# Early feed-forward weights in half-size tiles on the ScalarE queue, five instead of seven expert buffers, early work over all eight expert pairs

## The chip, the cores and the metric

The kernel runs on one core of a Trainium2 chip. The metric is the device time of one execution in microseconds (us). Times of a kernel are the median of several executions; one more execution is profiled, and all rows below come from that one.

## The reference

Two transformer blocks on 256 tokens of 1024 channels, in float32. The part that matters here is a mixture of experts at the end of the first block (16 experts, hidden size 512, two chosen per token) and, at the start of the second block, a feed-forward layer on the 256 context tokens, which do not depend on the first block.

```python
for e in range(N_EXPERTS):
    hidden = jax.nn.silu(xt @ w_exp_gate[e]) * (xt @ w_exp_up[e])
    y = y + combine[:, e:e + 1] * (hidden @ w_exp_down[e])
...
a, b = jnp.split(h @ w_up, 2, axis=-1)
return (jax.nn.silu(a) * b) @ w_down
```

## The kernel before

The stage in question is `moe` (lines 967 to 1031). It takes the tokens of each expert in slots of 64 and works on the experts in eight pairs; pairs are numbered 0 to 7 here. A pair (loop in `experts`, line 1139 on) needs twelve weight chunks of 1 MB: four of the gate, four of the up and four of the down matrices, one of each for expert `a=0` and one for `a=1`. In the profile their tile is `raw`, and their loads stand on the queue of SP (line 214).

For each pair TensorE (PE) runs, in the names of the rows:
- `egu` (line 1152): 32 matmuls, gate and up, in four groups of eight; a group reads two chunks. The matmuls of `a=0` and `a=1` alternate; each uses 64 of the 128 columns of the array, one the lower and one the upper half.
- `es`: ScalarE (ACT) takes the silu (line 1162), VectorE (DVE) the product (line 1163); `ept` (line 1166) transposes it, and DVE copies it to `hT` (line 1169).
- `ey` (line 1178): 16 matmuls, down, in two groups of eight on two chunks each; then ACT and DVE split the result into `y` high and low (lines 232, 233).
- `eo` (lines 1192, 1193): 16 matmuls that scatter `y` back to the tokens.
- in every second pair `gsp` and `gtp` (slot gates), and `xgp` (lines 1108 to 1111), 32 matmuls that gather the next four experts' tokens.

One matmul of `egu` or `ey` in the program is two rows in the profile (512 `egu` rows for 256 matmuls).

Between them stands **early work**: the second part (six of 22 hidden tiles) of the context tokens' feed-forward layer, which is independent of the experts. `early_ffn` (line 1037) is a generator: 24 steps for twelve up tiles (24 matmuls `pab` each) and 8 for the down tiles (18 matmuls `pd` each), 128x256 per matmul. `self.fill(n)` takes n steps. A weight tile is copied to a high part by ACT (line 225) and its rest taken by DVE (line 228) before PE reads it as `w`. Nine steps are taken ahead of pair 0, six in each pair from then on, and what is left in pair 5 (line 1018); after that the early work is done.

After pair 5 comes a loop that is entered only if an expert has more than 64 tokens (`values_load`, line 1022, and the branches after it); with these inputs it is skipped. The chunks of pair 6 that have a buffer are asked for ahead of it.

The order inside each engine is set by a scheduler of the framework, which places the instructions between two branches by its own estimates. A table of what stands where is given below.

Buffers: all weights of the stage share a ring of seven raw buffers of 1 MB (`raw` with 3, `rawm` with 4), experts and early weights alike; two more spare tiles hold chunks of pair 0. A load waits on its queue until the buffer's last reader is done.

Of the kernel before, what the change touches and what calls it, by code (L numbers as in the profile page):

```python
# [8 lines left out]
F32 = mybir.dt.float32  # L9
F32R = mybir.dt.float32r  # L10
I32 = mybir.dt.int32
AF = mybir.ActivationFunctionType
ALU = mybir.AluOpType
# [4 lines left out]
KD = 8  # L18
S = 256
T2 = 512  # L20
EPS = 1e-6
NFF = 22
PARTS = (6, 6, 6, 4)
EARLY = 1
LOOP_AT = 5
AHEAD = 5
FILL = 3
NORM_LAG = ((1, 3, 0, 2), (1, 2, 0, 3))
LATE_LAG = (2, 2)
# [140 lines left out]
class Builder:  # L170
# [796 lines left out]
    def moe(self):  # L967
        nc, I = self.nc, self.I
        V = nc.vector
        self.raw_n, self.raws = 0, 7  # L970
        with self.sub("hn", 1) as Q, self.sub("hide", PARTS[EARLY]) as E, self.sub("moe", 1) as P, \
                self.sub("wspe", 2) as self.wsp, self.sub("moew", 1) as W, self.sub("rawm", 4) as self.raw_more:
            hH = [Q.tile([128, 1024], F32R, name=f"hnH{t}") for t in range(2)]
            hL = [Q.tile([128, 1024], F32R, name=f"hnL{t}") for t in range(2)]
            rs = self.rs
            self.early = self.early_ffn(E)
            self.fill(FILL)
            comb, sel = self.route(self.lg, rs, P)
            self.fill(FILL)
            pp = self.mm("pos")  # L980
            nc.tensor.matmul(pp[:, 0:16], self.before, sel[:, 0, :], start=True, stop=True)
            nc.tensor.matmul(pp[:, 16:32], self.before, sel[:, 1, :], start=True, stop=False)
            nc.tensor.matmul(pp[:, 16:32], self.ones, sel[:, 0, :], start=False, stop=True)
            for t in range(2):
                nc.tensor.matmul(pp[:, 32:48], self.ones, sel[:, t, :], start=(t == 0), stop=(t == 1))
            mc = P.tile([128, 1], F32, name="mc")
            V.tensor_reduce(mc, pp[:, 32:48], AX.X, ALU.max)
            mi = P.tile([128, 1], I32, name="mi")
            V.tensor_scalar(mi, mc, -1.0, None, ALU.add)
            V.tensor_scalar(mi, mi, 6, None, ALU.logical_shift_right)  # L990
            pos = P.tile([128, 2, 16], F32, name="pos")
            V.scalar_tensor_tensor(pos, pp[:, :32].rearrange("p (t e) -> p t e", t=2), 1.0, sel,
                                   ALU.add, ALU.mult)
            V.tensor_scalar(pos, pos, -1.0, None, ALU.add)
            for t in range(2):
                for q in range(2):
                    p = self.a2("hnt")[:, 0, :] if q else self.mm("hnt")
                    for j in range(4):
                        nc.tensor.transpose(p[:, j * 128:(j + 1) * 128],
                                            self.h[:, q * 4 + j, t * 128:(t + 1) * 128], self.ident)  # L1000
                    hi, lo = hH[t][:, q * 512:(q + 1) * 512], hL[t][:, q * 512:(q + 1) * 512]
                    nc.scalar.activation(hi, p, AF.Copy, scale=rs[:, t:t + 1])
                    V.scalar_tensor_tensor(lo, p, rs[:, t:t + 1], hi.bitcast(F32), ALU.mult, ALU.subtract)
            self.fill(FILL)
            self.gates_of_route()
            order = [(p, c) for p in range(8) for c in range(12)]
            ready = {pc: self.expert_chunk(*pc) for pc in order[:AHEAD]}
            self.spare = [P.tile([128, 2048], F32, tag="xg", name="raw", bufs=2),
                          W.tile([128, 2048], F32, tag="y", name="raw")]
            ready.update({pc: self.expert_chunk(*pc) for pc in order[AHEAD:AHEAD + 2]})  # L1010
            self.on_pool = 0
            self.gs = P.tile([128, 8], F32, name="gs")
            pos2 = P.tile([128, 2, 16], F32, name="pos2")
            V.tensor_copy(pos2, pos)
            for p in self.experts(pos, comb, hH, hL, P, W, ready):
                if p != LOOP_AT:
                    continue
                for _ in self.early:
                    pass
                ready.update({(p + 1, c): self.expert_chunk(p + 1, c) for c in range(7)})  # L1020
                with self.tc.issue_after(self.loaded.ins):
                    more = nc.values_load(mi[0:1, 0:1], min_val=0, max_val=3)
                self.raw_loop = self.wsp
                with self.tc.If(more > 0):
                    with self.tc.For_i(0, more, 1):
                        V.tensor_scalar(pos2, pos2, -64.0, None, ALU.add)
                        for _ in self.experts(pos2, comb, hH, hL, P, W, {}):
                            pass
                self.raw_loop = None
            self.raw_more = None  # L1030
        self.pending = self.two_norms(self.sums)

# [1 line left out]
        for _ in range(n):  # L1034
            next(self.early, None)

    def early_ffn(self, E):
        nc, I = self.nc, self.I
        up, dn = I["ffn1_up_2"][0], I["ffn1_down_2"][0]
        f0, nf = sum(PARTS[:EARLY]), PARTS[EARLY]  # L1040
        sl = slice(S, 2 * S)
        hid = []

        def fetch(c):
            c0 = (f0 + 2 * c) * 128
            return [self.rows(up, 0, KD, m + c0, 256) for m in (0, NFF * 128)]

        nxt = fetch(0)
        for c in range(nf // 2):
            cur, nxt = nxt, fetch(c + 1) if 2 * c + 2 < nf else None  # L1050
            for i in range(2):
                p = self.mm("pab")
                for m in range(2):
                    w = self.split_w(cur[m][:, :, i * 128:(i + 1) * 128])
                    for ks in (range(4), range(4, KD)):
                        self.gemm(p[:, m * S:(m + 1) * S], w, self.xact(sl), ks=ks)
                        if m == 0 or ks[0] == 0:
                            yield True
                s, t = self.s512("fs")[:, :S], self.s512("ft")[:, :S]
                nc.scalar.activation(s, p[:, :S], AF.Silu)  # L1060
                nc.vector.tensor_tensor(t, s, p[:, S:], ALU.mult)
                hid.append([E.tile([128, S], F32R, tag=x, name=x) for x in ("eH", "eL")])
                self.split_a(*hid[-1], t)
                yield True
        for dc in range(4):
            v = self.rows(dn, f0 * 128, nf, dc * 256, 256)
            for i in range(2):
                w = self.split_w(v[:, :, i * 128:(i + 1) * 128])
                p = self.mm("pd")[:, :S]
                self.gemm(p, w, lambda f: hid[f])  # L1070
                self.residual(p, 2 * dc + i, 0, 0, 1)
                yield True

    def expert_chunk(self, p, c):
        I = self.I
# [7 lines left out]
    def experts(self, pos, comb, hH, hL, P, W, ready):  # L1083
        nc, I = self.nc, self.I
# [6 lines left out]
        def chunk(p, c):  # L1091
            w = ready.pop((p, c), None)
            return w if w is not None else self.expert_chunk(p, c)
# [47 lines left out]
        for p in range(8):  # L1141
# [4 lines left out]
            for m in range(2):  # L1146
                for kh in range(2):
                    for aa in both:
                        w = {a: chunk(p, m * 4 + kh * 2 + a) for a in aa}
                        for kk in range(4):  # L1150
                            for a in aa:
                                mm(pr[a * 64:a * 64 + 64, m, :],  # L1152
                                   xg[p // 2][:, kh * 4 + kk, es[a] % 4 * 64:es[a] % 4 * 64 + 64], w[a][:, kk, :],
                                   start=(kh == 0 and kk == 0), stop=(kh == 1 and kk == 3))
                    if self.raw_loop is None:
                        self.fill(1)
            if p % 2 == 0:
                slot_gates(p // 2)
# [2 lines left out]
            s = self.s512("es")  # L1161
# [9 lines left out]
            for fh in range(2):  # L1171
                for aa in both:
                    w = {a: chunk(p, 8 + fh * 2 + a) for a in aa}
                    for ff in range(2):
                        f = fh * 2 + ff
                        for n in range(2):
                            for a in aa:
                                mm(y[a * 64:a * 64 + 64, n, :], hT[:, f, a * 64:a * 64 + 64],
                                   w[a][:, ff, n * 512:(n + 1) * 512], start=(f == 0), stop=(f == 3))
                if self.raw_loop is None:  # L1180
                    self.fill(1)
            y2 = W.tile([128, 2, 1024], F32R, tag="y", name="y")
            yH, yL = y2[:, 0, :], y2[:, 1, :]
# [600 lines left out]
```

## Time and profile before

| | us |
|---|---|
| median of 3 runs | 2293.41 (2293.08 to 2294.7) |
| profiled execution | 2290.45 |
| its span, on core 0 | 2288.6 |
| first `egu` of pair 0 | 313.71 |
| last `eo` ahead of the loop | 543.98 |
| first `egu` behind the loop (pair 6) | 558.34 |
| `sums`, behind the last `eo` of pair 7 | 617.86 |

The span is the time between the first and the last instruction on the core. A row of the timeline gives the start, the length, the engine, the line, the operation, what it writes and reads, and how many equal instructions were merged; in brackets stands how long the engine was idle ahead of it and what ended that. Windows give the busy time of each engine in a stretch, the granted TensorE clock as a share of 2.4 GHz, the busy share of the 16 DMA engines and what they moved.

### The profile page before, as it was taken

Reading aid. Unit: us, or ns where it says so; the run is one execution under the profiler, and the core shown is the slowest. Engines: PE = TensorE matmul, PEld = TensorE weight load, DVE = VectorE, ACT = ScalarE, POOL = GpSimd, SP = SyncE. Lnnn points to the kernel's source line nnn. Section 1 sums busy time; section 2 is a strip of 40 time slices with the busy share of each in tenths; the row PEclk is TensorE's granted clock in tenths of the full one; section 3 lists DMA queues with packets and bytes.
Section 4 is the critical chain, followed back from the end, with each engine's and each line's share of the span. In section 5 each row is a group of like instructions: output and inputs, shape, how many; then the busy total and the mean of one; then the engine's idle time right before and its main releaser. Section 6 shows DMA issues by size and latency. Waiting matters only on the chain.

```text
span 2288.6 us, 32426 instructions
## 1 busy us (share of the span) xinstructions
PE 2217.9 (97%) x13295; PEld 1815.5 (79%) x13295; DVE 1439.2 (63%) x2516; ACT 816.5 (36%) x1256; POOL 163.0 (7%) x160
## 2 busy tenths in 40 slices
PE   8999999998899999999999999999999999899998
PEld 8789974643488977877897777789778888879998
DVE  5656842221388778766678777737874335877676
ACT  4554431110132322346642222224222223485443
POOL 0200100000000000330220000001000002312000
PEclk9999999998899999999999999999999999999999
DMA  7673858897946755320135555434653222416551
GB/s 253 214 241 129 275 191 317 320 395 313 367 162 206 230 171 169 93 85 28 56 130 190 192 170 183 139 96 136 194 165 111 87 70 69 113 33 221 185 175 47
DMA packets 273173, 395.91 MB, mean 173 GB/s; under 512 B 18156, under 2 KB 220540, under 8 KB 260604
## 3 DMA queue, kind: packets, MB, share of 16 engines
q1 hardware_dynamic: 272000, 392.33, 50.7%
q8 instruction: 106, 1.74, 0.3%
q0 software_dynamic: 576, 1.18, 0.2%
q14 instruction: 47, 0.39, 0.1%
q10 hardware_dynamic: 444, 0.27, 0.0%
HBM read 392.71 MB, written 1.05 MB: 172 GB/s over the span
## 4 chain that ended last, share of the span: by engine, by line
PE 69%; DVE 5%; ACT 1%; POOL 1%; issue 1%; ACTq 0%; DVEq 0%; POOLq 0%
PE pab L241 12%; PE pab L242 12%; PE pab L243 12%; PE pd L241 6%; PE pd L242 6%; PE pd L243 6%; PE pj L242 1%; PE pj L241 1%; PE pj L243 1%; PE egu L1152 1%; PE aT L1637 1%; PE as L1608 1%; DVE xL L330 1%; PE ao L1654 1%; PE ada_ps L521 1%; PE po L241 1%
## 5 line engine op out<-in xcount | busy, mean ns | idle before, releaser
L225 ACT ACTIVATE w<-raw 128x1024 fp32r<-128x1024 f32 (+2 forms) x432 | 425.7, 990 | 695.2 <-PE pd L243 239.5
L228 DVE TENSOR_TENSOR w<-raw,w 128x1024 fp32r<-128x1024 f32 (+2 forms) x422 | 479.1, 1145 | 184.7 <-ACT w L225 182.8
L242 PE MATMUL pab<-xL,w 128*128 128x512 f32 (+2 forms) x1600 | 552.3, 346 | 2.3 <-DVE xL L330 1.0
L241 PE MATMUL pab<-xH,w 128*128 128x512 f32 (+2 forms) x1600 | 553.2, 346 | 0.2
L243 PE MATMUL pab<-xH,w 128*128 128x512 f32 (+2 forms) x1600 | 552.0, 345 | 1.4 <-POOL w L228 1.4
L241 PEld LDWEIGHTS pab<-xH,w 128*128 128x128 f32 x1600 | 303.3, 190 | 55.4 <-issue 9.9
L243 PEld LDWEIGHTS pab<-xH,w 128*128 128x128 f32 x1600 | 303.2, 190 | 44.4 <-issue 3.2
L242 PEld LDWEIGHTS pab<-xL,w 128*128 128x128 f32 x1600 | 303.2, 190 | 44.1 <-DVE xL L330 2.3
L539 DVE SCALAR_TENSOR_TENSOR acc<-raw,sT,acc 128x512 f32<-128x512 f32 x420 | 284.8, 745 | 0.0
L241 PE MATMUL pd<-hH,w 128*128 128x512 f32 (+1 forms) x800 | 267.8, 337 | 0.1
L242 PE MATMUL pd<-hL,w 128*128 128x512 f32 (+1 forms) x800 | 267.8, 336 | 0.0
L243 PE MATMUL pd<-hH,w 128*128 128x512 f32 (+1 forms) x800 | 267.1, 335 | 0.0
L241 PE MATMUL pj<-xH,w 128*128 128x256 f32 (+1 forms) x816 | 250.7, 309 | 11.1 <-DVE qra L1536 4.7
L242 PE MATMUL pj<-xL,w 128*128 128x256 f32 (+1 forms) x816 | 246.0, 302 | 6.1 <-DVE xL L330 5.3
L243 PE MATMUL pj<-xH,w 128*128 128x256 f32 (+1 forms) x816 | 245.1, 301 | 0.5 <-DVE w L228 0.5
L241 PEld LDWEIGHTS pj<-xH,w 128*128 128x128 f32 x816 | 156.1, 192 | 26.7 <-DVE qra L1536 5.5
L241 PEld LDWEIGHTS pd<-hH,w 128*128 128x128 f32 x800 | 151.8, 191 | 20.1 <-ACT fs L636 3.4
L686 DVE SCALAR_TENSOR_TENSOR h<-pd,gmod,h 128x256 f32<-128x256 f32 x224 | 100.8, 479 | 104.9 <-PE pd L243 104.6
L242 PEld LDWEIGHTS pj<-xL,w 128*128 128x128 f32 x816 | 156.9, 192 | 11.9 <-DVE xL L330 6.6
L243 PEld LDWEIGHTS pd<-hH,w 128*128 128x128 f32 x800 | 152.3, 191 | 16.8 <-issue 1.7
L242 PEld LDWEIGHTS pd<-hL,w 128*128 128x128 f32 x800 | 152.4, 191 | 15.4 <-DVE hL L233 0.2
L243 PEld LDWEIGHTS pj<-xH,w 128*128 128x128 f32 x816 | 156.8, 192 | 5.7 <-DVE w L228 0.8
(388 smaller groups left out, 2490.3 us busy)
## 6 DMA issues: line engine op xcount, KB each, us to landing
raw<-ffn_up SPq DMA_DIRECT2D x94, 1024.0 KB, 5.4
raw<-w_ada SPq DMA_DIRECT2D x72, 1024.0 KB, 5.3
raw<-ffn_down SPq DMA_DIRECT2D x52, 768.0 KB, 4.8
raw<-w_in SPq DMA_DIRECT2D x32, 1024.0 KB, 5.4
raw<-w_exp_gate SPq DMA_DIRECT2D x32, 1024.0 KB, 8.4
raw<-w_exp_up SPq DMA_DIRECT2D x32, 1024.0 KB, 8.0
raw<-w_exp_down SPq DMA_DIRECT2D x32, 1024.0 KB, 7.5
raw<-w_gate SPq DMA_DIRECT2D x8, 1024.0 KB, 5.8
```

Source lines behind the costliest of these rows:

```text
L225: self.nc.scalar.activation(wh, v, AF.Copy)
L228: e.tensor_tensor(wl, v, wh.bitcast(F32), ALU.subtract)
L241: mm(o, wH[:, k, :], aH, start=(first and k == 0), stop=False)
L242: mm(o, wH[:, k, :], aL, start=False, stop=False)
L243: mm(o, wL[:, k, :], aH, start=False, stop=(last and k == n - 1))
L330: nc.vector.scalar_tensor_tensor(lo, t, B(j), hi.bitcast(F32), ALU.add, ALU.subtract)
L521: mm(ps[g * 32:(g + 1) * 32, :], self.unit[:, 31 - r:63 - r], acc[v], start=(u < 2), stop=(u > 3))
L539: ins = V.scalar_tensor_tensor(acc[v], w[:, g, :], s, acc[v], ALU.mult, ALU.add)
L686: self.nc.vector.scalar_tensor_tensor(hs, p, self.gmod[:, l, n, d, v:v + 1], hs, ALU.mult, ALU.add)
L1152: mm(pr[a * 64:a * 64 + 64, m, :], xg[p // 2][:, kh * 4 + kk, es[a] % 4 * 64:es[a] % 4 * 64 + 64], w[a][:, kk, :], start=(kh == 0 and kk = ...
L1608: mm(o[:, c], qs, x[i][:, c], start=(i == 0 and not (near and c.start == 0)), stop=(i == 1))
L1637: nc.tensor.transpose(T[:, j * 128:(j + 1) * 128], e[:, a, j * 128:(j + 1) * 128], self.ident)
```

## The change

- The early weights no longer share the experts' ring. They get four own buffers of half the size (`rawe`, 512 KB); a tile holds 128 columns instead of 256, so that there are 20 loads in place of 10, with rows of 512 bytes in place of 1 KB. They are issued from ACT's queue: the first four at the start of the early work, each further one behind the split of the tile that was taken from the list.
- The experts' ring has five buffers instead of seven (`raw` with 3, `rawm` with 2), and five chunks instead of seven are asked for ahead of the loop.
- `fill` is called after the second half of the gate, of the up and of the down matmuls only: three steps in each pair instead of six. What would be drained in pair 5 goes on in pairs 6 and 7; ahead of the loop only a tile in the midst of its work is finished.

```diff
+EARLY_BUFS = 4
...
-        self.raw_n, self.raws = 0, 7
+        self.raw_n, self.raws = 0, 5
...
-                self.sub("wspe", 2) as self.wsp, self.sub("moew", 1) as W, self.sub("rawm", 4) as self.raw_more:
+                self.sub("wspe", 2) as self.wsp, self.sub("moew", 1) as W, self.sub("rawm", 2) as self.raw_more, \
+                self.sub("rawe", EARLY_BUFS) as R:
...
-                for _ in self.early:
-                    pass
-                ready.update({(p + 1, c): self.expert_chunk(p + 1, c) for c in range(7)})
+                while self.early_open:
+                    self.fill(1)
+                ready.update({(p + 1, c): self.expert_chunk(p + 1, c) for c in range(self.raws)})
...
+            for _ in self.early:
+                pass
...
-            return [self.rows(up, 0, KD, m + c0, 256) for m in (0, NFF * 128)]
...
+        def fetch(w, r0, k, c0):
+            v = R.tile([128, 1024], F32, tag="fw", name="raw")[:, :k * 128].rearrange("p (k c) -> p k c", c=128)
+            nc.scalar.dma_start(v, w[r0:r0 + 128 * k, c0:c0 + 128].rearrange("(k p) c -> p k c", p=128))
+            return v
+
+        todo = [(up, 0, KD, m + (f0 + f) * 128) for f in range(nf) for m in (0, NFF * 128)]
+        todo += [(dn, f0 * 128, nf, d * 128) for d in range(KD)]
+        got = [fetch(*todo.pop(0)) for _ in range(EARLY_BUFS)]
+
+        def weights():
+            w = self.split_w(got.pop(0))
+            if todo:
+                got.append(fetch(*todo.pop(0)))
+            return w
...
-                    if self.raw_loop is None:
+                    if self.raw_loop is None and kh:
                         self.fill(1)
...
-                if self.raw_loop is None:
+                if self.raw_loop is None and fh:
                     self.fill(1)
```

What the scheduler makes of it, at three places. (All lines of the changed kernel lie higher by 1 or more: 1152 is now 1166, 1166 is 1180, 1178 is 1192.)

PE, the end of the gate and up matmuls of pair 1 and the start of its down matmuls; `pab` is early work, `ept` the transposes that wait for `es`. Before:

```order
L241 MATMUL pab<-xH,w 128x256
L242 MATMUL pab<-xL,w 128x256
L1152 MATMUL egu<-raw,xg 64x512 x7
L243 MATMUL pab<-xH,w 128x256
L1152 MATMUL egu<-raw,xg 64x512 x16
L1166 MATMUL ept<-sqc,es 128x128 x4
L241 MATMUL pab<-xH,w 128x256
```

And now:

```order
L243 MATMUL pab<-xL,w 128x256
L244 MATMUL pab<-xH,w 128x256
L1166 MATMUL egu<-raw,xg 64x512 x7
L1180 MATMUL ept<-sqc,es 128x128 x4
L1192 MATMUL ey<-raw,hT 64x512 x16
L1166 MATMUL egu<-raw,xg 64x512
L1206 MATMUL eo<-xL,y 128x256
```

The early matmuls between `ept` and `ey` have gone from this pair, and the last sixteen `egu` are now cut by early work into seven, one and seven with the one ahead of them.

PE, the gate and up matmuls of pair 6, behind the loop. Before, with the last gather row and the slot gates:

```order
L1111 MATMUL xgp<-xH,hnL_3109 128x256
L1152 MATMUL egu<-raw,xg 64x512 x32
L1132 MATMUL gsp<-rt_comb,xH 64x1 x4
L1135 MATMUL gtp<-sqc,xH 128x128 x2
L1132 MATMUL gsp<-rt_comb,xH 64x1 x4
L1135 MATMUL gtp<-sqc,xH 128x128 x2
L1166 MATMUL ept<-sqc,es 128x128 x4
```

And now, from behind the first sixteen `egu` and the eighteen `pd` (early work) that follow them:

```order
L1166 MATMUL egu<-raw,xg 64x512 x9
L242 MATMUL pd<-eH,w 128x256
L243 MATMUL pd<-eL,w 128x256
L244 MATMUL pd<-eH,w 128x256
L242 MATMUL pd<-eH,w 128x256
L243 MATMUL pd<-eL,w 128x256
L244 MATMUL pd<-eH,w 128x256
L242 MATMUL pd<-eH,w 128x256
L243 MATMUL pd<-eL,w 128x256
L244 MATMUL pd<-eH,w 128x256
L242 MATMUL pd<-eH,w 128x256
L1166 MATMUL egu<-raw,xg 64x512 x7
```

One unbroken run of 32 has become three, of 16, 9 and 7.

SP's queue ahead of the loop (`TENSOR_LOAD` is the `values_load`). Before:

```order
L214 DMA raw<-w_exp_up 128x2048 x4
L214 DMA raw<-w_exp_down 128x2048 x4
L214 DMA raw<-w_exp_gate 128x2048 x4
L214 DMA raw<-w_exp_up 128x2048 x3
L1022 TENSOR_LOAD mi
```

And now:

```order
L215 DMA raw<-w_exp_up 128x2048 x4
L215 DMA raw<-w_exp_down 128x2048 x4
L215 DMA raw<-w_exp_gate 128x2048 x4
L215 DMA raw<-w_exp_up 128x2048
L1024 TENSOR_LOAD mi
```

Two chunks of pair 6 have moved behind the loop.

## Rows read from the trace of the kernel before

**Rows 1.** The page: busy time by engine, and the chain that ended last.
```profile
PE 2217.9 (97%) x13295; PEld 1815.5 (79%) x13295; DVE 1439.2 (63%) x2516; ACT 816.5 (36%) x1256; POOL 163.0 (7%) x160
...
PE 69%; DVE 5%; ACT 1%; POOL 1%; issue 1%; ACTq 0%; DVEq 0%; POOLq 0%
```
**Rows 2.** Windows of 20 us: busy by engine, PE clock, DMA share, GB/s.
```profile
360.00:380.00 20.00, 19.32 (x108) 11.01 (x108) 5.32 (x7) 3.75 (x5) 0.00 (x0) 1.00 0.73 266
...
500.00:520.00 20.00, 17.13 (x82) 7.19 (x84) 5.30 (x8) 1.50 (x3) 0.00 (x0) 1.00 1.01 418
```
**Rows 3.** The waits of PE, 313 to 618 us: total us, times, longest.
```profile
PE ept L1166 <- DVE es L1163: 6.7, 5, 1.5
...
PE eo L1193 <- DVE y L233: 4.3, 9, 0.9
PE ey L1178 <- DVE hT L1169: 3.1, 4, 0.8
PE eo L1192 <- ACT y L232: 1.4, 2, 0.7
PE egu L1152 <- DMA raw<-w_exp_up: 0.7, 1, 0.7
```
**Rows 4.** PE's timeline in pairs 3 and 5: expert runs of several lengths.
```profile
455.62 1.07 PE L1152 MATMUL egu<-raw,xg 128*64 128x512 f32 x2
456.62 0.38 PE L243 MATMUL pd<-eH,w 128*128 128x256 f32 x1
...
458.54 3.65 PE L1152 MATMUL egu<-raw,xg 128*64 128x512 f32 x14
462.11 0.39 PE L243 MATMUL pd<-eH,w 128*128 128x256 f32 x1
462.43 3.65 PE L1152 MATMUL egu<-raw,xg 128*64 128x512 f32 x16
...
514.11 13.95 PE L1152 MATMUL egu<-raw,xg 128*64 128x512 f32 x62
```
**Rows 5.** PE's timeline in pair 3: eighteen early matmuls, and what runs behind them.
```profile
447.21 0.39 PE L241 MATMUL pd<-eH,w 128*128 128x256 f32 x1
...
449.47 3.65 PE L1152 MATMUL egu<-raw,xg 128*64 128x512 f32 x16
```
**Rows 6.** PE's timeline in pairs 4 and 5: two kinds of wait, two `ey` runs.
```profile
501.14 0.74 PE L1166 MATMUL ept<-sqc,es 128*128 128x128 f32 x4 [1.47 <-DVE es L1163]
502.67 7.09 PE L1178 MATMUL ey<-raw,hT 128*64 128x512 f32 x32 [0.78 <-DVE hT L1169]
...
531.06 8.78 PE L1178 MATMUL ey<-raw,hT 128*64 128x512 f32 x32 [0.79 <-DVE hT L1169]
```
**Rows 7.** The DMA view: a chunk's landing time, one alone and twelve in a stream.
```profile
raw<-w_exp_up SPq DMA_DIRECT2D x1, 1024.0 KB, 4.8
raw<-w_exp_gate SPq DMA_DIRECT2D x12, 1024.0 KB, 10.2
```
**Rows 8.** Shorter windows, columns as in rows 2: transfer rate, and the clock.
```profile
532.00:536.00 4.00, 4.00 (x14) 1.26 (x12) 0.00 (x0) 0.00 (x0) 0.00 (x0) 0.59 1.02 422
576.00:580.00 4.00, 4.00 (x12) 1.19 (x14) 0.00 (x0) 0.00 (x0) 0.00 (x0) 0.57 1.02 422
...
620.00:630.00 10.00, 10.00 (x51) 10.00 (x51) 4.87 (x24) 1.50 (x2) 0.00 (x0) 0.53 1.07 368
...
564.00:572.00 8.00, 8.00 (x40) 2.69 (x37) 0.00 (x0) 0.00 (x0) 0.00 (x0) 1.00 1.00 424
...
544.00:558.30 14.30, 7.92 (x35) 7.65 (x33) 3.44 (x7) 1.42 (x3) 0.00 (x0) 0.64 0.38 152
```
**Rows 9.** Timelines of ACT and DVE: a load's issue, a tile's copy, its rest.
```profile
1.18 0.46 ACTq L485 DMA_DIRECT2D vrows<-vec_rows  x1
...
365.81 1.05 ACT L225 ACTIVATE w<-raw 128x1024 fp32r<-128x1024 f32 x1
...
366.89 1.23 DVE L228 TENSOR_TENSOR w<-raw,w 128x1024 fp32r<-128x1024 f32 x1 [0.53 <-ACT w L225]
```

More of the change, by code (lines that the diff above doesn't have):

```diff
@@ L975, in moe @@
             rs = self.rs
-            self.early = self.early_ffn(E)
+            self.early = self.early_ffn(E, R)
             self.fill(FILL)
@@ L1035, in fill, with early_ffn @@
             next(self.early, None)
-    def early_ffn(self, E):
+    def early_ffn(self, E, R):
         nc, I = self.nc, self.I
@@ L1042, in early_ffn @@
         hid = []
-        def fetch(c):
-            c0 = (f0 + 2 * c) * 128
-            return [self.rows(up, 0, KD, m + c0, 256) for m in (0, NFF * 128)]
[L1048 to L1072, printed above, removed]
+        self.early_open = True
+        def fetch(w, r0, k, c0):
+            v = R.tile([128, 1024], F32, tag="fw", name="raw")[:, :k * 128].rearrange("p (k c) -> p k c", c=128)
+            nc.scalar.dma_start(v, w[r0:r0 + 128 * k, c0:c0 + 128].rearrange("(k p) c -> p k c", p=128))
+            return v
@@ new lines, in early_ffn @@
+        todo = [(up, 0, KD, m + (f0 + f) * 128) for f in range(nf) for m in (0, NFF * 128)]
[6 more added lines that the diff above has]
+            return w
+        for f in range(nf):
+            p = self.mm("pab")
+            for m in range(2):
+                w = weights()
+                for ks in (range(4), range(4, KD)):
+                    self.gemm(p[:, m * S:(m + 1) * S], w, self.xact(sl), ks=ks)
+                    if m == 0 or ks[0] == 0:
+                        yield True
+            s, t = self.s512("fs")[:, :S], self.s512("ft")[:, :S]
+            nc.scalar.activation(s, p[:, :S], AF.Silu)
+            nc.vector.tensor_tensor(t, s, p[:, S:], ALU.mult)
+            hid.append([E.tile([128, S], F32R, tag=x, name=x) for x in ("eH", "eL")])
+            self.split_a(*hid[-1], t)
+            self.early_open = False
+            yield True
+            self.early_open = True
@@ L1074, in expert_chunk @@
+        for d in range(KD):
+            w = weights()
+            p = self.mm("pd")[:, :S]
+            self.gemm(p, w, lambda f: hid[f])
+            self.residual(p, d, 0, 0, 1)
+            self.early_open = False
+            yield True
     def expert_chunk(self, p, c):
```

## The prediction, made before the changed kernel ran

> **What bounds the kernel now.** Read the page first. PE is busy for 97% of the span and holds 69% of the chain that ended last [rows 1]; the stage that changes gives work to PE, to ACT and DVE, and to the DMA engines, so the next view is the windows. Early in the stage PE works without a break and the DMA engines have room; late in it, where the early work has ended, they are full at 418 GB/s and PE still has holes [rows 2]. One would guess that the transfers make the holes. The waits say no: a load held PE once, for 0.7 us, while the gate's product `es` took 6.7 us in five waits, its transposed copy `hT` 3.1 in four, and the split of `y` 5.7 in eleven [rows 3]. These, with 0.3 at the sums, are PE's 16.5 us of idle time in the stage outside the loop's gap. So PE sets the pace by what it executes and by three small waits in a pair. Of the change I count the work on PE, the three waits, new waits for transfers, and the clock.
>
> **Work on PE: the cost of a cut.** An expert run of seven program matmuls (14 rows) takes from 458.54 to 462.11, 3.57 us; one of eight takes 3.65 as a row, which is the row of seven to the digit; a single one takes 1.00; 31 take 13.95 [rows 4]. So the two halves of the array run side by side: a run costs 0.86 us for each pair of matmuls, an odd one counted as a pair, and 0.14 for its end (31 are 16 slots: 13.9). Early matmuls cost 0.118 us each and 0.2 a run: 18 took 2.26 us, from 447.21 to 449.47 [rows 5], and a single one 0.32 [rows 4].
>
> Now count on PE's order, from the first `egu` to the sums. Expert runs go from 42 to 52, and the odd ones among them lift the slots from 205 to 211: 6 × 0.86 + 10 × 0.14 = 6.6 us. Early runs go from 26 to 40, with 324 matmuls in place of 323: 14 × 0.2 + 0.1 = 2.9. The scatter `eo` has two runs more: 0.3. Together **+9.8 us**. At least 5.3 of it are sure, the odd slots and the matmul, even if every end were hidden under what follows.
>
> In the pairs this is no even spread. The work ahead of the loop falls by 7 us, since 90 of the 144 `pd` leave it; behind it, pairs 6 and 7 take 17 more: the 90 matmuls (10.6 us), and cuts in runs that were whole. It is the cuts that cost; moving a matmul alone is neutral.
>
> **The three waits.** An uncovered wait for `es` costs 1.47 us and one for `hT` 0.78 [rows 6]; it is covered where early or expert matmuls stand between producer and consumer in the order. After the change early work stands ahead of the transposes in pairs 0, 2 and 6; in pairs 1, 3, 4, 5 and 7 nothing does: 5 × 1.47 = 7.3 against 6.7. `hT` stays open in four pairs. For `y`, matmuls move beside the split in three pairs and leave it in others; I get 5.3 against 5.7. The one load wait of 0.7 goes into the next term. Net **−0.5 us**. Bounds: zero, and −4.4 if three of the five `es` waits were covered after all.
>
> **Transfers with five buffers.** The stream gives 424 GB/s [rows 8], 2.5 us for a chunk; a chunk alone lands 4.8 us after its issue [rows 7]. An unbroken run of 31 uses eight chunks in 13.9 us, 1.7 each, faster than the stream. With seven buffers it ran without a stop [rows 4]. Now take pair 3, which by the order keeps such a run, with five. Chunks 4 and 5 are wanted at 6.9 us; chunk 5 gets its buffer when the first group of eight ends, at 3.5, and lands at 8.3: PE waits 1.4. Chunk 7 gets its buffer at 7, lands behind chunk 6 at 13.3, and PE wants it at 11.8: 1.5. In pair 4, half cut, the same sum gives 0.9. **+4 us.** Bounds: 0, if the chunks are all there when the run starts and land faster than a lone one; 10, if pairs 3, 4 and 5 each pay for two chunks and the next gate as well. Behind the loop five chunks are ready instead of seven; cuts by 18 and 10 early matmuls stretch pair 6's groups, so I expect no wait.
>
> The 20 half-size tiles carry the same 10 MB. Twelve chunks in a stream took 10.2 us each to land [rows 7], yet the rate stayed at 424 GB/s: the part of a landing that is not transfer, 4.8 − 2.5 = 2.3 us, overlaps the next one. So I take nothing for the doubled count; unoverlapped, ten more tiles would be 23 us of the queues' time, about 11 of it in the tight pairs 3 to 5. That is a rival below. The Trainium skill ("DMA: Bandwidth & Descriptors", Anatomy of one DMA) speaks against small tiles: it gives each DMA about 2 us fixed, besides its bytes, and puts half efficiency near 860 KB. By that rule 512 KB tiles would run at under half of the rate and the sum would be that rival's; the stream of rows 7 and 8 says that the fixed part does not add up. No row shows a transfer with 512-byte rows in this pattern. By the same page (Specifications) 512 bytes is just enough for the full rate, so it would add nothing.
>
> **The clock.** Twice PE ran at about half of 2.4 GHz in late pairs, at 532 (0.59) and 576 (0.57) [rows 8]; the `ey` of pair 5 took 8.78 us where pair 4's took 7.09 [rows 6]: 1.7 us each. In the pair 4 row the same waits went by without a drop, so it is no fixed price of a wait. Early work makes pairs 6 and 7 denser, and pair 5 emptier: I take one drop gone, **−1.7 us**. Bounds: two more drops, +3.4; and below, all of them gone, with the slow gather behind the loop's gap (0.64, at most half of 7.92 busy us: 4.0) and the slow start of the next layer (10 us at 0.53: 4.7) [rows 8]: −12.1. The gap itself has no early work in it now either, so the gather should stay slow.
>
> **The queues.** Twenty loads move to ACT's queue. An issue there takes 0.46 us, and it stands behind the tile's copy (1.05) and waits for DVE's rest (1.23) [rows 9], so ACT is held for up to 1.7 us a tile; thirteen of them lie behind the first `egu`. ACT is busy for 36% of the span [rows 1], and PE reads the tile only behind the rest, so I take 0. In pairs 1, 2, 4 and 5 a load stands right ahead of the silu; late by a microsecond each, that would be +4. SP loses these loads; what else it issues moves with it. The next layer's first weights are asked for some 7 us later: 0, at most +2.
>
> **Sum:** 9.8 − 0.5 + 4 − 1.7 = +11.6 us. The profiled execution of before took 2290.45 us (span 2288.6 and 1.85 around it) and becomes 2302.1; the median lies 3.0 above it, so **2305.0**. A change of 0.2%, 4.6 us, is what a measurement of this kernel can tell from none.
>
> **The rivals.**
>
> *The clock pays for it.* Place: the `ey` of pairs 5 and 6, the gather, the start of the next layer; price 3.4 + 4.0 + 4.7 = 12.1 us. If the early matmuls in pairs 5 to 7 keep PE at 2.4 GHz throughout, and five buffers do, the sum is 9.8 − 0.5 − 12.1 = −2.8, 2290.6, not slower. It decides from 5 us of regained clock, given no load waits. For it: the drops stand where early work was lacking. Against it: pair 4 lacked it too, and the gap stays. The Trainium skill ("TensorE: Matmul & The Clock Gate", Part 1) has the low clock as the default which activity lifts; by it the drops would all go where the holes fill up. The row of pair 4 agrees only in part. Chance 0.15.
>
> *The same, and the ends of runs are hidden.* Then the work is 5.3: 5.3 − 0.5 − 12.1 = −7.3, 2286.1, faster. Against it: the lone matmuls of rows 4 pay their ends in full. Chance 0.10.
>
> *The transfers bind.* Half-size tiles with short rows slow the stream that has no room in pairs 4 and 5 [rows 2]; five buffers don't ride it out. +11 on top: 22.6, 2316.0. It decides once a pair takes longer to fetch than PE needs. Against it: the rate held in a stream of many transfers. Chance 0.17.
>
> That the change does nothing is excluded by the order: the cuts are there.
>
> **How the numbers follow.** The forecast has 0.58. Its own range goes from +3 (no load waits, 2.5 less of run ends and clock) to +20 (load waits of 10, two late queues), most of it above +4.6. Slower: 0.58 + 0.17 = 0.75; same 0.15; faster 0.10. The range leaves out the fastest tenth and the upper half of the transfers' rival: 2289.5 to 2318.
>
> **What would show it.** The profile after should have pab and pd between the `egu` and `ey` runs of pairs 6 and 7; single `egu` rows of 1.0 us; the last `eo` ahead of the loop some 5 us earlier or less, where load waits eat it, and the sums 10 to 14 us later; waits for `raw` by a DMA in pair 3, some 3 us; `es` waits of 1.47, five. The forecast is wrong if waits by DMA exceed 10 us (transfers), if no window between 313 and 632 shows a clock below 0.9 (clock), or if single matmuls show less than 0.9.

## The result, and the profile after

| | before | after |
|---|---|---|
| median, us | 2293.24 | 2310.4 (2307.08 to 2313.37, 4 runs) |
| ratio to before | | 1.0084 (95%: 1.0062 to 1.0106) |
| span of the profiled execution | 2288.6 | 2306.1 |
| first `egu` to the gap behind pair 5 | 230.6 | 230.5 |
| that gap and the gather, to the first `egu` of pair 6 | 14.1 | 12.8 |
| pairs 6 and 7, to the sums | 59.5 | 74.7 |
| sums to the end of the span | 1670.7 | 1674.6 |

The change costs 14 to 24 us by the interval, 17.5 in the profiled spans. The forecast was +11.6 and 2305.0, its range 2289.5 to 2318: sign right, the size short by 6 us in the profile.

The page of the changed kernel looks the same, as in [rows 1]. PE is still the bound, and what was added is in it:

```profile
PE 2226.5 (97%) x13295; PEld 1819.3 (79%) x13295; DVE 1444.3 (63%) x2516; ACT 817.0 (35%) x1256; POOL 164.5 (7%) x160
...
PE 69%; DVE 5%; ACT 1%; POOL 1%; issue 1%; DMA 0%; DVEq 0%; SPq 0%; ACTq 0%; POOLq 0%
```

PE's busy time in the two parts of the stage is read from windows (columns as in [rows 2]; the second figure is PE). Before:

```profile
313.70:544.26 230.56, 220.84 (x1144) 114.82 (x1143) 57.72 (x92) 32.11 (x52) 0.00 (x0) 0.99 0.87 342
558.30:617.80 59.50, 52.70 (x253) 20.52 (x252) 11.14 (x18) 7.06 (x12) 0.00 (x0) 0.97 0.90 353
```

After:

```profile
313.40:543.90 230.50, 212.77 (x1055) 105.10 (x1054) 49.89 (x82) 29.43 (x48) 0.00 (x0) 1.00 0.87 335
556.80:631.30 74.50, 67.53 (x343) 31.69 (x342) 16.70 (x26) 9.61 (x14) 0.00 (x0) 0.99 0.81 309
```

PE's work ahead of the loop fell by 8.1 us and yet that part did not get shorter; behind the loop it rose by 14.8. The first is explained by PE's waits, 17.6 us ahead of the loop against 9.7 before. For the whole stage, the view of [rows 3] on the changed kernel shows:

```profile
PE ept L1180 <- DVE es L1177: 8.2, 6, 1.5
PE egu L1166 <- DMA raw<-w_exp_up: 5.9, 3, 2.7
PE xgp L1122 <- DVE xH L1111: 5.1, 1, 5.1
PE eo L1207 <- DVE y L234: 4.0, 9, 0.9
PE ey L1192 <- DVE hT L1183: 3.4, 4, 1.0
PE eo L1206 <- ACT y L233: 3.1, 4, 1.0
PE sums L1218 <- ACT sq L1212: 0.2, 1, 0.2
```

Without the line of `xgp`, which is the gap, 24.8 us stand here against 16.5 before: 5.2 more for chunks, 1.5 for `es`, 0.3 for `hT`, 1.4 for `y`. The waits for chunks are where the sum put them, in the unbroken run of pair 3 and in pair 4. PE's timeline there:

```profile
444.86 3.68 PE L1166 MATMUL egu<-raw,xg 128*64 128x512 f32 x16 [1.88 <-DMA raw<-w_exp_up]
449.84 3.65 PE L1166 MATMUL egu<-raw,xg 128*64 128x512 f32 x14 [1.30 <-DMA raw<-w_exp_up]
455.02 0.75 PE L1180 MATMUL ept<-sqc,es 128*128 128x128 f32 x4 [1.53 <-DVE es L1177]
...
488.03 3.65 PE L1166 MATMUL egu<-raw,xg 128*64 128x512 f32 x14 [2.69 <-DMA raw<-w_exp_up]
...
501.60 1.02 PE L1166 MATMUL egu<-raw,xg 128*64 128x512 f32 x2
```

Pair 3 waited 1.88 and 1.30 us where 1.4 and 1.5 were worked out, pair 4 2.69 where 0.9 was. The matmul at 501.60 is a single one: it holds PE for the 1.0 us that the sum gave it.

PE's time per matmul is unchanged but for the clock. The `ey` groups of the stage, before and then after:

```profile
L1178 PE MATMUL ey<-raw,hT 128*64 128x512 f32 x256 | 62.7, 626 | 3.1 <-DVE hT L1169 3.1
```

```profile
L1192 PE MATMUL ey<-raw,hT 128*64 128x512 f32 x256 | 60.3, 597 | 3.4 <-DVE hT L1183 3.4
```

The 626 ns became 597, the two slow runs of [rows 8] are gone: −2.4 us by this group. So the busy time, +6.8 in all, is about +9.2 of work and −2.4 of clock. Adding up busy time times (1 − clock) over windows of 4 us agrees: 3.0 us were lost in the stage before and 0.5 after.

Behind the sums the clock is worse than before. Windows of 4 us there, after:

```profile
631.50:635.50 4.00, 4.00 (x19) 4.00 (x20) 1.70 (x2) 3.35 (x5) 0.00 (x0) 0.50 0.79 243
...
643.50:647.50 4.00, 4.00 (x23) 4.00 (x22) 3.86 (x30) 0.00 (x0) 0.00 (x0) 0.56 1.02 365
647.50:651.50 4.00, 4.00 (x36) 4.00 (x36) 1.31 (x5) 0.55 (x2) 0.00 (x0) 1.00 0.78 256
```

PE ran at the lower level, 1.2 GHz, for about 16 us from just ahead of the sums on, against 10 to 12 us before [rows 8]. The same tally from the sums on gives 7.8 us lost after and 5.1 before. That is 2.7 of the 3.9 us by which the rest of the span grew; the other 1.2 us are not placed.

### The profile page after: what moved, and what is told of

Same layout as the page of the kernel before. It is cut to its first block, busy times and chain, and to the rows that moved or that the text cites. A ratio compares the mean times of both kernels' runs of the same rounds, so it can differ in the third digit from the quotient of the medians.

```text
span 2306.1 us, 32444 instructions
## 1 busy us (share of the span) xinstructions
PE 2226.5 (97%) x13295; PEld 1819.3 (79%) x13295; DVE 1444.3 (63%) x2516; ACT 817.0 (35%) x1256; POOL 164.5 (7%) x160
## 4 chain that ended last, share of the span: by engine, by line
PE 69%; DVE 5%; ACT 1%; POOL 1%; issue 1%; DMA 0%; DVEq 0%; SPq 0%; ACTq 0%; POOLq 0%
PE pab L242 12%; PE pab L243 12%; PE pab L244 12%; PE pd L242 6%; PE pd L243 6%; PE pd L244 6%; PE pj L243 2%; PE pj L244 1%; PE pj L242 1%; DVE xL L331 1%; PE egu L1166 1%; PE aT L1651 1%; PE as L1622 1%; PE ao L1668 1%; PE ada_ps L522 1%; PE po L242 1%
```

## The experiments

**Parts of the change.** Four kernels ran together, with the kernel before beside them. My theory was then: the loss is made by cut runs and by five buffers, not by the spread. Rival: the spread, with work behind the loop, makes it.

The tiles alone; the early work in its old places:

```diff
-                while self.early_open:
-                    self.fill(1)
+                for _ in self.early:
+                    pass
...
-                    if self.raw_loop is None and kh:
+                    if self.raw_loop is None:
...
-                if self.raw_loop is None and fh:
+                if self.raw_loop is None:
```

> The new loads and buffers alone: early weights in half-size tiles on ACT's queue, five expert buffers, but early work filled in and drained as before (six steps a pair, nothing behind the loop). Theory (half-size tiles and five buffers make the loss): by the order of PE its work is 5.5 us more than before (more odd expert runs, 35 early runs for 26) and the es, hT and y waits 1.9 more; pairs 4 to 6 keep unbroken runs of 23 and 31 with five buffers, so 3 to 8 us of waits for chunks. Together +10 to +15: 2303 to 2308. Rival (the spread makes the loss): within 5 us of before, 2288 to 2298.

Measured: 2311.12 us, ratio 1.0097 (1.0081 to 1.0112): as slow as the whole change, and 3 us above the range expected. Chunks were waited for longer than expected, in pair 4, pair 5 and behind the loop too. Its first two lines of waits:

```profile
PE egu L1164 <- DMA raw<-w_exp_up: 9.2, 6, 3.0
PE ept L1178 <- DVE es L1175: 7.9, 6, 1.5
```

The rival, no loss without the spread, falls.

The spread alone, with the old tiles in the ring of seven:

```diff
-                for _ in self.early:
-                    pass
+                while self.early_open:
+                    self.fill(1)
...
-                    if self.raw_loop is None:
+                    if self.raw_loop is None and kh:
...
-                if self.raw_loop is None:
+                if self.raw_loop is None and fh:
```

> The spread alone: three early steps a pair, the rest behind the loop, but 256-column early tiles in the ring of seven on SP's queue as before. Theory: the order of PE shows no more work than before (272.9 against 273.2 us by the prices of runs), but seven es waits in place of five and all hT waits, +6.4 us; the early tiles hold ring buffers over more pairs, so waits for chunks of 0 to 10 us come on top: 2299 to 2310. Rival (cuts come with the spread, loads don't matter): +10 of work and no waits for chunks, egu rows of single matmuls as in the changed kernel: about 2303. Second rival (the clock stays up in pairs 5 to 7 and after the stage): 2290 or less.

Measured: 2315.43 us, 1.0108 (1.0088 to 1.0127), slower than expected. Not the cuts did it, but waits of `es` and of chunks, and the clock. From its waits:

```profile
PE ept L1172 <- DVE es L1169: 11.3, 8, 1.6
...
PE egu L1158 <- DMA raw<-w_exp_up: 6.4, 3, 3.0
...
PE ey L1184 <- DMA raw<-w_exp_down: 3.0, 2, 1.6
```

And its two parts of the stage:

```profile
313.13:557.38 244.25, 217.72 (x1072) 109.89 (x1071) 52.30 (x84) 28.80 (x48) 0.00 (x0) 0.96 0.81 317
571.86:643.37 71.51, 64.77 (x326) 29.23 (x325) 16.62 (x26) 10.29 (x16) 0.00 (x0) 0.95 0.82 316
```

PE was busy for 282.5 us here, 9.0 more than before; by the tally of the clock 11.9 us were lost in the stage against 3.0 before, so its work was the same, as the theory had it. All eight `es` waits stand, and even seven buffers run dry; early tiles that are used up at half the rate and so sit in ring buffers longer would explain that, which was not tried by itself. With the tiles' own buffers (the whole change) the spread costs nothing more than the tiles alone: each part loses by itself, and together they lose no more than one.

The whole change, but drained ahead of the loop:

```diff
-                while self.early_open:
-                    self.fill(1)
+                for _ in self.early:
+                    pass
...
-            for _ in self.early:
-                pass
```

> The whole change, but the early work that is left is drained in pair 5, ahead of the loop, as before. Theory (moving a matmul over the loop is neutral, cuts cost): by the order PE has 5.0 us less work than the changed kernel, and 2.5 more of es, hT and y waits; pair 6's egu run is whole again with five buffers, so 1 to 4 us of waits for chunks come there. In all 2306 to 2311, the part behind the loop back at 60 to 63 us (74.5 in the changed kernel, 59.5 before). Rival (work behind the loop is what costs): the part behind the loop shrinks by 15 us and the part ahead grows by less than 6, so 2301 or less.

Measured: 2310.63 us, 1.0089 (1.0075 to 1.0102), the whole change's time within 0.3 us. In sum, moving the 90 matmuls across the loop is neutral, as the theory had it. Its terms came out otherwise: PE's work, the clock taken out, was 2.3 us less in place of 5.0, and the waits for chunks were 9.9 us in the stage in place of 5.9. The part behind the loop was 66.9 us, where 60 to 63 was expected; its two longest waits:

```profile
PE egu L1164 <- DMA raw<-w_exp_up: 3.1, 3, 1.4
PE ept L1178 <- DVE es L1175: 2.9, 2, 1.5
```

In the changed kernel no chunk was waited for behind the loop. So early work in pair 6 had also been hiding late chunks there.

Six buffers, and two early tiles, in the same memory:

```diff
-EARLY_BUFS = 4
+EARLY_BUFS = 2
...
-        self.raw_n, self.raws = 0, 5
+        self.raw_n, self.raws = 0, 6
...
-self.sub("rawm", 2) as self.raw_more, \
+self.sub("rawm", 3) as self.raw_more, \
```

> The whole change, but six expert buffers and two early tiles of half size in place of five and four (the same memory). Theory (five buffers make the 5.9 us of waits for chunks, and some of the cuts): waits for chunks at most 2 us; by the order 3.2 us less work and 2.5 less of es, hT and y waits than the changed kernel: 2300 to 2304 beside the changed kernel's 2308 to 2313. Rival (the half-size tiles slow the stream): waits for chunks stay at 4 to 6 us and the time falls by less than 6 us; with two early tiles waits for w appear on PE.

Measured: 2301.35 us, 1.0048 (1.0033 to 1.0064), some 9 us less than the whole change and inside the range expected.

```profile
PE egu L1166 <- DMA raw<-w_exp_up: 1.4, 1, 1.4
```

With one more buffer 4.5 of the 5.9 us of waits for chunks are gone, with the same half-size tiles on the same queue; nothing waits for `w`. Two early tiles in place of four, and a somewhat other order on PE, come with it and were not tried alone. The rival of slow small tiles falls. The profiled run, 2295.08 us, was this kernel's fastest; even there PE is busy for 278.6 us in the stage, 5.1 more than before, which fits the cuts that are left (9.8 − 3.2 = 6.6 by the prices).

**The queue.** The early loads from POOL's queue:

```diff
-            nc.scalar.dma_start(v, w[r0:r0 + 128 * k, c0:c0 + 128].rearrange("(k p) c -> p k c", p=128))
+            nc.gpsimd.dma_start(v, w[r0:r0 + 128 * k, c0:c0 + 128].rearrange("(k p) c -> p k c", p=128))
```

> The changed kernel with the early loads issued from POOL's queue in place of ACT's; the order on PE is the same but for one matmul. Theory (an issue on ACT's queue delays the silu and the split of y a little): PE's waits ended by ACT fall from 3.1 us to about 1.4 and hT's longest from 1.0 to 0.8, the waits for chunks stay at 5 to 7 us; 2306 to 2311 beside the changed kernel's 2310. Rival (the queue matters): over 4 us faster, or slower by as much if POOL delays the early weights' rest or the issues.

Measured: 2313.47 us, 1.0094 (1.0072 to 1.0115). The ratio can't be told from the whole change's, though the time lies above the range expected, and my reason fell: PE's waits ended by ACT stayed at 3.1 us and `hT`'s longest at 1.0.

```profile
PE ey L1192 <- DVE hT L1183: 3.4, 4, 1.0
PE eo L1206 <- ACT y L233: 3.1, 4, 1.0
```

They don't come from issues on ACT's queue. The waits for chunks, 5.6 us, are the same as well, so in the stage no worth of the queue is seen. In the profiled run the stage began 6.2 us later (first `egu` at 319.73); why is not known.

**Placing the early work.** If cuts and open waits are the loss, the same steps tied to the waits must gain. The three steps of a pair go behind the last matmul of `egu`, the last `ept` and the last `ey`, and may not be taken up sooner (`issue_after` keeps an instruction behind another in its engine's order):

```diff
+    def fill_after(self, last):
+        if self.raw_loop is None:
+            with self.tc.issue_after(last.ins):
+                self.fill(1)
...
-                    if self.raw_loop is None and kh:
-                        self.fill(1)
...
+            self.fill_after(last)
             s = self.s512("es")
...
+            self.fill_after(last)
             y = self.a2("ey")
...
-                if self.raw_loop is None and fh:
-                    self.fill(1)
+            self.fill_after(last)
```

> The whole change, but with the three early steps of a pair put where PE waits: one behind the last gate and up matmul, one behind the transposes, one behind the last down matmul (each tied to the matmul it follows, by issue order). By the prices of runs PE's work falls to 266.5 us (283.2 in the changed kernel, 273.2 before) and the es, hT and y waits to 2 us (18.9 in the changed kernel). Theory (five buffers can't feed unbroken runs of 32): waits for chunks of 15 to 25 us, so 2283 to 2295. Rival (the loss lay in the cuts and uncovered waits alone): waits for chunks stay near 6 us, 2272 to 2280.

Measured: 2291.16 us, 0.9997 (0.9985 to 1.0009): the time of before, 19 us less than the whole change with the same loads and buffers and the same early work. All its waits in the stage:

```profile
PE egu L1171 <- DMA raw<-w_exp_up: 16.5, 11, 2.9
PE xgp L1127 <- DVE xH L1116: 7.0, 1, 7.0
PE ept L1184 <- DVE es L1181: 3.7, 1, 3.7
PE eo L1210 <- ACT y L233: 1.7, 2, 0.9
PE eo L1211 <- DVE y L234: 1.1, 2, 0.9
```

Of six `es` waits one is left, `hT`'s are gone, and whole runs ask for chunks faster than five buffers give them, 16.5 us, as expected; `es` and `y` took 6.5 us, though, where 2 were expected. Without the gap these waits come to 23.0 us against 24.8 in the changed kernel, since the waits for chunks took nearly all that the others gave. The gain, 16.7 us between the two profiled spans, is mostly PE's busy time:

```profile
314.70:531.85 217.15, 201.04 (x1055) 104.27 (x1054) 49.00 (x80) 29.04 (x48) 0.00 (x0) 0.99 0.90 351
546.52:618.38 71.86, 64.95 (x343) 31.52 (x342) 16.64 (x27) 9.77 (x15) 0.00 (x0) 0.96 0.82 320
```

PE was busy for 266.0 us in place of 280.3. With the clock taken out (3.8 us lost here, 0.5 there) that is 17.7 us less for the same matmuls, and the prices of runs gave 16.7. So between these two kernels it was the cuts that cost.

Then the same with six buffers and two early tiles:

> The same placing with six expert buffers and two early tiles. Theory: work 266.6 us and es, hT and y waits of 2 us as with five buffers; waits for chunks 5 to 15 us, 5 to 10 less than with five: 2273 to 2286, faster than before. Rival (the stream of 106 MB at 2.5 us per MB, 265 us, sets the pace whatever the buffers): the time of the kernel with five buffers within 3 us, and waits for chunks over 15 us.

Measured: 2283.99 us, 0.9969 (0.9953 to 0.9984): faster than the kernel before. Waits for chunks fell to 9.3 us.

```profile
PE egu L1171 <- DMA raw<-w_exp_up: 9.3, 6, 2.6
```

It is the buffers, not the stream's total, that hold PE: the rival with the five buffers' time falls. (Here too the early tiles went from four to two.)

**The tail and the clock.** Here 7.6 us were lost to the clock behind the sums, by the tally used above. A step kept for pair 7's `y`:

```diff
-            self.fill(FILL)
+            self.fill(FILL - 1)
             self.gates_of_route()
```

> As the one before, but one early step less is taken ahead of pair 0, so that one is left for the wait for y in pair 7, the last work of the stage. Theory (the slow clock at the start of the next layer follows the holes at the end of the stage): by the order the y waits fall by 1.7 us, and the stretch below 0.9 of the clock behind the sums gets shorter than the 12 us of before, so 2 to 5 us less than the kernel before it in this set. Rival: the slow stretch comes all the same, and the time is within 2 us of it.

Measured: 2283.52 us, 0.9964 (0.9947 to 0.998): within 0.5 us of the placed kernel, as the rival said, yet the slow stretch behind the sums did shrink, to 3.4 us lost. A second `es` wait came in its place (7.0 us in two, against 3.7 in one), and ahead of the loop the clock took 5.3 us by the tally, against 3.1 in the placed kernel.

To keep the work ahead of pair 0 as it was, the spare step was taken from pair 3 instead:

```diff
-            self.fill_after(last)
+            if p != 3:
+                self.fill_after(last)
             y = self.a2("ey")
```

> The placed kernel with six buffers, without the early step behind the transposes of pair 3, so that one step is left for the wait for y in pair 7; nothing is taken from the work ahead of pair 0. By the order: the hT wait of that pair opens again, 0.8 us, the y waits at the end of the stage fall by 1.7. Theory (holes at the end of the stage bring the slow clock at the start of the next layer; the kernel with the tail step lost 3.4 us there, all others 5 to 8): the loss there is 3 to 4 us again, so 3 to 6 us less than the placed kernel: 2278 to 2282. Rival (the loss there comes and goes by itself): 6 to 8 us, and the time within 2 us of 2284.

Measured: 2281.51 us, 0.9961 (0.9947 to 0.9975), the lowest ratio of the study, 0.4% below before. It lies in the range expected, but the intervals of the three placed kernels with six buffers overlap. The second `es` wait is there as well. The clock behind its sums:

```profile
611.20:615.20 4.00, 4.00 (x28) 4.00 (x28) 2.93 (x4) 3.37 (x5) 0.00 (x0) 0.75 1.05 378
615.20:619.20 4.00, 4.00 (x20) 4.00 (x21) 3.02 (x20) 0.00 (x0) 0.00 (x0) 0.50 1.09 348
619.20:623.20 4.00, 4.00 (x32) 4.00 (x32) 2.01 (x16) 0.00 (x0) 0.00 (x0) 0.90 1.06 375
```

Lost here: 4.00 × (0.25 + 0.5 + 0.1) = 3.4 us. In the placed kernel without the step, with `y` waits of 0.2 to 1.1 us open in pair 7, the clock was low for 16 us:

```profile
607.80:611.80 4.00, 3.96 (x19) 3.96 (x19) 1.83 (x3) 3.44 (x5) 0.00 (x0) 0.50 0.77 240
...
615.80:619.80 4.00, 4.00 (x21) 4.00 (x21) 2.31 (x7) 0.00 (x0) 0.00 (x0) 0.50 1.08 361
619.80:623.80 4.00, 4.00 (x23) 4.00 (x23) 3.86 (x28) 0.00 (x0) 0.00 (x0) 0.59 1.02 364
```

In both kernels whose tail holds early work the loss is 3.4 us; in the nine others profiled, before and after among them, it is 5.1 to 7.8. The link holds in every profile, but it is no more than that: in these two a wait for the sums' squares (2.2 and 2.4 us) opened right ahead of the sums, so an open wait there does not by itself bring the whole loss. Why it stays at 3.4, and whether that wait is the cause, was not tried.

## Why the prediction was right, and where it was short

- **Work on PE, +9.8:** +9.2 by the busy time, the clock taken out. The price of runs, from a few rows of the kernel before, gave the right sum and nearly the right places: ahead of the loop 7 less was counted and 6.5 less came, behind it 17 more was counted and 15.9 came.
- **Transfers, +4:** the waits for chunks rose by 5.2. Pair 3 came out as worked out, pair 4 was mis-sized, 2.7 for 0.9: I let its cuts count as time in which chunks arrive, but the second part of its run was 23 matmuls whole. With a sixth buffer 1.4 us were left.
- **The three waits, −0.5:** this step failed. They rose by 3.2. `es` rose by 1.5 where 0.6 was counted: the half-open wait of pair 6 (0.76), which I had as covered, stood as it had before. `hT` rose by 0.3, and the split of `y` by 1.4 where −0.4 was counted. Of that, 1.0 is a single new wait in pair 7, for ACT's second half of `y`:

```profile
625.65 0.50 PE L1206 MATMUL eo<-xL,y 128*128 128x256 f32 x2 [0.72 <-ACT y L233]
...
628.36 0.50 PE L1206 MATMUL eo<-xL,y 128*128 128x256 f32 x2 [1.00 <-ACT y L233]
```

The other waits of pair 7, 0.72, 0.23 and 0.87, stood there before as well (0.70, 0.23 and 0.85). ACT's rows tell where the new one comes from, first before, then after:

```profile
613.15 0.60 ACT L232 ACTIVATE y<-ey 128x512 fp32r<-128x512 f32 x1 [9.50 <-PE ey L1178]
613.65 1.05 ACT L225 ACTIVATE w<-raw 128x1024 fp32r<-128x1024 f32 x1
614.59 0.59 ACT L232 ACTIVATE y<-ey 128x512 fp32r<-128x512 f32 x1
```

```profile
625.00 0.60 ACT L233 ACTIVATE y<-ey 128x512 fp32r<-128x512 f32 x1 [9.53 <-PE ey L1192]
626.76 1.06 ACT L226 ACTIVATE w<-raw 128x1024 fp32r<-128x1024 f32 x1 [1.16 <-DMA raw<-ffn_up]
627.72 0.58 ACT L233 ACTIVATE y<-ey 128x512 fp32r<-128x512 f32 x1
```

Between the halves of `y` stands the copy of the next layer's first weight tile, and it now waits 1.16 us for its load. That load was issued 15.7 us ahead of the sums before and 9.9 us ahead now, and the second half of `y` starts 2.72 us behind the first in place of 1.44.
- **The clock, −1.7:** right in kind inside the stage (both drops went, −2.4 together, where one was counted), but short behind it. I had put the slow start of the next layer only into a bound on the gain side; its loss grew by 2.7. Taken together the clock gave nothing. The Trainium skill ("TensorE: Matmul & The Clock Gate", Part 1) has the low clock as the default that activity lifts; the runs agree in so far as early work in the tail cut the loss from 7.6 to 3.4 us.
- **The gap behind pair 5, 0:** −1.3 us, since `xH` came 1.3 sooner. Not foreseen, and small.
- **Queues, 0:** held for the loads on ACT's queue (eleven were issued from the first `egu` on, where thirteen were counted); with POOL's queue in its place the same waits stand. For SP's queue 0 was short: the next layer's weights, asked for some 6 us later, are the wait of 1.0 us in pair 7, inside the bound of 2.
- **Sum:** 9.2 + 5.2 + 3.2 − 2.4 = +15.2 in the stage (+15.1 by the parts), −1.3 for the gap, +3.9 behind, −0.2 for its first `egu`: 17.5. The terms are off by +3.9, +3.7 and +1.2 to one side and by −1.3, −0.7, −0.6 and −0.2 to the other, so a part of the misses cancels.

The rival of **transfers that bind** because the tiles are small did not happen: with the same tiles and six buffers 1.4 us of waits for chunks were left. Yet the small tiles were not free. Over the stage (310 to 632, 322 us) SP's queue (q1) and the early tiles' (q10) show packets, MB and the share of time that the packets took on the 16 DMA engines:

```profile
q1 hardware_dynamic: 15424, 96.47, 76.9%
q10 hardware_dynamic: 9392, 4.72, 5.1%
```

That is 390 GB/s for the chunks and 287 for the early tiles: 16.4 us for eleven tiles, where 12.1 would do at the chunks' rate. The 4.3 us, 0.4 a tile, are for the doubled count and the short rows together; what each is worth is not shown. With POOL's queue the rate was much the same, 5.40 MB, other loads of POOL among them, in 5.3% of 332 us. The Trainium skill ("DMA: Bandwidth & Descriptors", Anatomy of one DMA) gives a fixed 2 us for each DMA, on the path of loads that GpSimd issues; the trace, where ACT issues them and a tile costs 0.4 us more, differs from a reading in which these 2 us would add up in a stream.

The two rivals in which **the clock pays** had the drops inside the stage right. They were lost to its tail, and the gather behind the gap stayed slow: 2.6 us were lost there before and 2.9 after, by the tally. That the ends of runs are hidden, which the second of them needs, is out too: 9.2 us of work came, not 5.3.

## What to carry to other kernels

Count runs, not matmuls: where an engine runs two halves side by side, work that cuts a run at an odd place cost about a microsecond a cut here. The same work tied to the engine's own waits made no such cuts: 17.7 us less of work, and some 19 us between two kernels with the same loads, buffers and matmuls. A buffer ring that suffices at a broken pace is short at an unbroken one, so the two must be changed together. Look at the last waits of a stage: the clock of the next one may hang on them, and its first loads can lengthen them.

## What was not expected of the hardware

In the kernel before and in the changed one, a run of waits of 0.2 to 1.0 us at the end of the stage is followed by 10 to 16 us at 1.2 GHz, although PE never stops in these 10 to 16 us; with early work in the place of those waits it was 6 to 8 us. And a wait for a chunk, 2.7 us in a pair, left the clock at 1.00 all through pairs 3 to 5 of the changed kernel, while the kernel with the spread alone lost 11.9 us to the clock in the stage.
